# Rotated stores on another queue, and the output's first operand in two transfers with its low parts last

## The chip, the cores and the metric

The kernel runs on one core of a Trainium2 chip. The metric is the device time of one execution in microseconds (us), lower is better. The kernel before was timed in three runs; the profile comes from a separate execution, taken with the hardware profiler.

## The reference, cut to what matters

One decoder block on a sequence of 2048 positions and 1024 channels, in float32:

```python
proj = h @ w_in[l]                      # eight parts of 1024 columns
x_rnn, z_rnn, q, k, v, z_attn, g_r, g_a = jnp.split(proj, IN_SPLITS, axis=-1)
hr = rg_lru(causal_depthwise_conv(x_rnn, ...), ...)
y_rnn = (hr * silu(z_rnn)) @ w_out_rnn[l]
qh = apply_partial_rope(q.reshape(B, S, N_HEADS, HEAD_DIM), cos, sin)   # 32 of a head's 128 columns turn
kh = apply_partial_rope(k.reshape(B, S, N_HEADS, HEAD_DIM), cos, sin)
o = dilated_attention_mixture(qh, kh, vh).reshape(B, S, D_ATTN)
y_attn = (o * silu(z_attn)) @ w_out_attn[l]
merged = sigmoid(g_r + bg_r) * y_rnn + sigmoid(g_a + bg_a) * y_attn
x = x + gate[:, None, :] * (merged @ w_o[l])
return rms_norm(x, g_final)
```

What matters here is the turn from `proj` to the attention and to the product with `w_out_rnn`, whose input, hr times silu(z_rnn), is the tensor `yaT`.

## The kernel before

**Numbers.** Every float32 operand is split into a high part (rounded, by ScalarE, `hi_act`, line 162) and a low part (the rest, by GpSimd, `lo_pool`, line 168, or VectorE, `lo_dve`, line 171). A product of two operands is three matmuls on TensorE (`mm3`): high by high, high by low, low by high. All matmuls have line 154. On TensorE's part of the profile, "LDWEIGHTS" (PEld) loads a 128 by 128 block and "MATMUL" (PE) streams 512 columns past it.

**Projections.** They run in two passes over halves of the sequence (`f` = 0, then 1). In a pass there are 28 pairs of column blocks, in the order of `pair_order`; each pair is one Strassen step of seven products (`strassen`), and a product is twelve matmuls (four blocks of the contraction, three matmuls each). The seven products of a pair read the operands B11, T2, T3, T1, B21, T4 and B22 of the normalised input, each as a high and a low tile `T`. Those tiles lie in a pool of 14 slots; a slot is free for another tile when the last pair's product has read it, B11's two slots first. The last product of a pair (B22) is issued behind the first of the next pair. The counter `n_prod` counts issued products over both passes, 196 in each. Work that goes with the products is put into lists by that count: `steps_after` and `late` for steps of evictions, `after_prod` for others; `run_late` runs what is due after each product, first `late`, then `after_prod`, then the operands of coming pairs (`pump`).

The weights are tiles `S` in a ring of seven slots. In the second pass most come back ready split from the scratch `sD`, by SyncE's queue (SP, line 334), and some raw, split four products ahead of their use; those of the pairs 22 and 27 (the last one) are built anew: raw loads `R` (line 257), sums on VectorE (lines 298 to 312), high parts on ScalarE and low parts on GpSimd.

**Evictions.** A pair gives four tiles of 128 by 512. The last six pairs of a pass are plain q, rotated q, plain, rotated k, plain, plain (`TAIL_ROTATED`). A rotated tile goes through a shuffle (VectorE, line 1157), two products (GpSimd, line 1158, and VectorE, line 1161), a sum (VectorE, line 1165) and a store of four transfers, one for each head's 32 rows (line 1170), the sum and the store being one product apart. A plain tile is stored in two or so transfers (line 1200). An eviction that needs no sum is made by ScalarE (line 1134), the others by VectorE (line 482). All these stores are issued by SP. ScalarE's queue issues the stores of `oD` in the second pass (lines 1353 and 1354), the scaled `w_o`, which is loaded as `wo` by SP (line 1335).

**Queues.** SP and ScalarE issue their transfers in the order of the program and wait, at each, for what it needs. ScalarE's transfers stand in line with its arithmetic. The compiled program gives each transfer one of eight completion semaphores in turn, in program order over both queues, so a transfer also waits until the eighth before it has landed.

**The turn.** After the product that frees the slot of a weight tile, `load_free` calls `load_next`. When the 196 weights of the pass are through, it goes on with what the output needs: the first weights of `w_out_rnn` from the scratch `wD` into the first slots of the ring (`load_wd`, line 367), four 128 by 512 tiles of `yaT` into the slots `R` (`load_yd`, line 373), and, at the second call, the other four blocks of `yaT` in one transfer into a slot `T` (line 345). It begins behind the last pair's second product (T2), when the last of that pair's weights is made.

**The output.** `steps` is a generator of output tiles: for each tile, eight blocks of the contraction, three matmuls each, into a PSUM tile `pj`. It is spent in pieces between the parts of the attention: the first 18 blocks, two tiles and a quarter, come before the attention's first scores. Ahead of the first tile, `split_y(0, k)` splits the eight blocks of the first operand, high part `yh` on ScalarE, low part `yl` on VectorE. Each tile takes two weight tiles of the ring's four slots, one for each half of the contraction; the load into a slot (`load_w`, again line 367) waits until TensorE has read the tile that was there. In the first tile the three matmuls of a block stand together: high, high by low, low by high.

**The attention** loads k and q of a head (`kraw`, lines 1522 and 1523), splits them into `kq`, and its first scores need the first of four such parts, its second group of scores all four. Its tiles are laid over the slots that the projections used: k's and q's second and third loads lie over the slot `T` that held the four blocks of `yaT`, and the buffers of `yh` lie in part over those of `wo`.

Of the kernel before, what the change touches and what calls it, by code (L numbers as in the profile page):

```python
# [10 lines left out]
F32 = mybir.dt.float32  # L11
# [9 lines left out]
P = 128  # L21
# [68 lines left out]
def decoder_block(ctx, tc, x, c, positions, g_norm, w_mod, b_mod, w_in, b_gate, conv_w, conv_b,  # L90
# [4 lines left out]
    def T(pool, shape, dt, tag, **kw):  # L95
        cnt[0] += 1
        return pool.tile(shape, dt, tag=tag, name=f"{tag}_{cnt[0]}", **kw)
# [228 lines left out]
    def load_next():  # L326
        n = n_loaded[0]
        n_loaded[0] += 1
        if n < 28 * 7:
            t = s_tile([P, 2, KH, P])  # L330
            if is_raw(n // 7, n % 7):
                unsplit.append((n, t, loaders[n // 7](*PLAIN[n % 7])))
            else:
                nc.sync.dma_start(t[:].bitcast(F32), sD[n])
            loaded.append((n, t))
        else:
            k = n - 28 * 7
            if k < 3:
                load_wd(0, 0, k) if k < 2 else load_wd(0, 1, 0)
            if k < 4:  # L340
                load_yd(yaT, 0, k)
            if k == 1:

                t = T(hp, [P, KH, CH], F32, "T", bufs=14)
                nc.sync.dma_start(t[:], yaT[KH * P :, :CH].rearrange("(k p) j -> p k j", p=P))
                for i in range(KH):
                    Y0[True, 0, KH + i] = t[:, i, :]


    def load_free():  # L350
        n = n_loaded
# [17 lines left out]
    def load_yd(ys, n, k):  # L369
        x = n_y[0]  # L370
        n_y[0] += 1
        t = T(pR, [P, CH], F32, f"R{x % 4}")
        nc.sync.dma_start(t[:], ys[k * P : (k + 1) * P, n * CH : (n + 1) * CH])
        Y0[ys is yaT, n, k] = t
# [767 lines left out]
    def rotated_pairs(qp, f, Ct, St):  # L1142

        for base, dstT, qs in QK:
            made = [0]

            def rotated(i, j, ps, u, dstT=dstT, qs=qs, made=made):
                n = 2 * f + j
                cq = slice(j * CH, (j + 1) * CH)
                t0 = T(qp, [P, CH], F32, "t0", bufs=NT0)  # L1150
                wait, v = scaled(t0, ps, u, qs), []
                wait += (0, 1, 2, 2)[made[0]]
                made[0] += 1

                def shuffle():
                    v.append(T(qp, [P, CH], F32, "t1", bufs=NT1))
                    nc.vector.stream_shuffle(v[0][:], t0[:], swap)
                    nc.gpsimd.tensor_tensor(t0[:], t0[:], Ct[:, cq], ALU.mult)

                def turn():  # L1160
                    nc.vector.tensor_tensor(v[0][:], v[0][:], St[:, cq], ALU.mult)

                def add():
                    t1 = v[0]
                    nc.vector.tensor_tensor(t1[:], t1[:], t0[:], ALU.add)

                def store():
                    for hh in range(4):
                        r0 = (4 * i + hh) * P
                        nc.sync.dma_start(dstT[r0 : r0 + 32, :, n * P : (n + 1) * P],  # L1170
                                          v[0][hh * 32 : (hh + 1) * 32, :].rearrange("p (r j) -> p r j", r=4))

                steps_after(n_prod[0], ((wait, shuffle), (wait + 1, turn), (wait + 2, add), (wait + 3, store)))

            strassen(qp, f, (base, "rotated"), rotated)
            yield
# [145 lines left out]
    def gated_weight(ep):  # L1322

        gate_b = T(ep, [P, D], F32, "gb")
        nc.sync.dma_start(gate_b[:], gateD[0:1, :].broadcast_to([P, D]))
        tt = nc.vector.tensor_tensor

        def group(k):
            v = {}

            def load():
                for i in range(2):
                    v[i] = T(ep, [P, 2, CH], F32, "wo", bufs=2)
                    rows = slice((i * KH + k) * P, (i * KH + k + 1) * P)
                    nc.sync.dma_start(v[i][:], w_o[0, rows, :].rearrange("p (j c) -> p j c", j=2))

            def gate(i):
                tt(v[i][:].rearrange("p j c -> p (j c)"), v[i][:].rearrange("p j c -> p (j c)"), gate_b[:], ALU.mult)

            def sums(i):  # L1340
                if not i:
                    v["t"] = T(ep, [P, 2, CH], F32, "ws")
                t = v["t"]
                (b11, b12), (b21, b22) = ((v[i][:, 0, :], v[i][:, 1, :]) for i in range(2))
                if not i:
                    tt(t[:, 0, :], b12, b11, ALU.subtract)
                    tt(t[:, 1, :], b22, t[:, 0, :], ALU.subtract)
                else:
                    tt(b22, b22, b12, ALU.subtract)
                    tt(b21, b21, t[:, 1, :], ALU.subtract)  # L1350

            def store_sums():
                nc.scalar.dma_start(oD[k, :, :2, :], v["t"][:])
                nc.scalar.dma_start(oD[k, :, 2:, :], v[1][:])

            return ((0, load), (4, lambda: gate(0)), (5, lambda: gate(1)), (6, lambda: sums(0)),
                    (7, lambda: sums(1)), (8, store_sums))

        for k, i in enumerate((1, 11, 21, 31)):
            for d, fn in group(k):  # L1360
                later(i + d, fn)
# [53 lines left out]
    for f in range(2):  # L1415
        if f:
            pools.close("xp")
            vx = pools.open("vx", bufs=1)
            second_values()
        else:  # L1420
            first_values()
        pools.close("vx")
        plain = plain_pairs(f)
        rp = pools.open("rp", bufs=1)
        touch(rp, (("u1", 1), ("u2", 2), ("u3", 1), ("xc", 2), ("y", 2), ("gi", 1), ("a", 1), ("t", 1),
                   ("gh", 1, 2, P), ("gl", 1, 2, P), ("xh", 1), ("xl", 1)))
        plain_pool[0] = rp
        plain_at[0] = lambda: T(rp, [P, CH], F32, "ev", bufs=3)
        bigr = reset_rows(rp, f)
        gates = gate_pairs(rp, f)  # L1430
        rotary_tables(rp, f)
        if f:
            output_weights()
            for x, (_, pieces) in enumerate(pair_order()):
                if x in ANEW:
                    events.extend((28 * 7 + 7 * x + d - LEAD, 15 * x + i, fn)
                                  for i, (d, fn) in enumerate(operand_events(x, pieces, f)))
            events.sort(key=lambda e: e[:2])

        pump()  # L1440
        n = 0
        for m in range(KT):
            recurrent(rp, bigr, f, m)
            for _ in range(others[m]):
                next(plain if is_plain(n) else gates)
                n += 1
        last_product()
        finish_late()
        pools.close("rp")
        qp = pools.open("qp", bufs=1)  # L1450
        plain_pool[0] = qp
        plain_at[0] = lambda: T(qp, [P, CH], F32, "t0", bufs=NT0)

        touch(qp, (("u1", 1), ("u2", 2), ("u3", 1), ("t0", NT0), ("t1", NT1)))
        tabs = load_tables(qp, f)
        if f:
            gated_weight(qp)
        else:
            xp = pools.open("xp", side="right", bufs=1)
            x0 = next_norm()  # L1460
        rotated = rotated_pairs(qp, f, *tabs)
        for n, r in enumerate(TAIL_ROTATED):
            if n == len(TAIL_ROTATED) - 1 and f == 0:
                next_even()
            next(rotated if r else plain)
        last_product()
        finish_late()
        for n in sorted(after_prod):
            run_late(n)
        pools.close("qp")  # L1470
# [341 lines left out]
    def steps(jobs):  # L1812
# [55 lines left out]
        def split_y(j, k):  # L1868
            if j < len(jobs):
                w, ys, n = jobs[j]  # L1870
                t = Y0.pop((ys is yaT, n, k), None)
                yh, yl = Y.get((j, k)) or new_y(j, k)
                t = yl[:].bitcast(F32) if t is None else t[:]
                hi_act(yh[:], t)
                on_dve = k not in (3, 4) if j == LAST_HEAD else k % 2 or not j
                (lo_dve if on_dve else lo_pool)(yl[:], t, yh[:])

        def load_g(t):
# [22 lines left out]
        for k in range(KT):  # L1901
            split_y(0, k)
        yield
        last = None
        for t, (j, m) in enumerate(tiles):
            ps = T(pj, [P, CH], F32, "pj") if j < LAST_HEAD or t % 4 < 2 else FP["bank"](t % 4 - 2)
            for k in range(KT):
# [18 lines left out]
                wt = W[x]  # L1926
                row = {5: 7, 6: 5, 7: 6}.get(k, k) if t == TURN + 1 else k
                yh, yl = Y[j, row]
                mm3(ps[:], wt[:, 0, row % KH, :], wt[:, 1, row % KH, :], yh[:], yl[:], first=k == 0, last=k == KT - 1)
                if k % KH == KH - 1 and (j != LAST_HEAD if m < KT - 1 else j <= LAST_HEAD):  # L1930
                    W.pop(x)

# [390 lines left out]
```

## Time and profile before

| | |
|---|---|
| median of three runs | 2206.31 us (2204.77 to 2211.26) |
| the profiled execution's own time | 2207.36 us |
| its span, first to last instruction | 2205.6 us |
| mean granted clock of TensorE | 0.993 |
| transfers | 513.90 MB, mean 233 GB/s |

Times in a profile are us from the start of the span. Rows of a timeline hold start, duration, engine, line, operation, output<-input, shapes, the number of merged instructions, and in brackets the idle time before and what ended it. "SPq" and "ACTq" rows are transfers being issued; the duration is that of the issue, not of the transfer. "DMA to landing" gives the time from issue until the last byte's semaphore (least, median, most). Rows of a waits view hold who waited for whom, us in total, times, the longest. Rows of the windows view hold the stretch, its length, the busy time and number of instructions of PE, PEld, VectorE (DVE), ScalarE (ACT) and GpSimd (POOL), the granted clock of TensorE, the mean busy share of the 16 DMA engines, and GB/s.

### The profile page before, as it was taken

To read this page: it belongs to the slowest core of one execution; us is meant where nothing else is said; L and a number is where in the kernel's file an instruction comes from. 1 tells how busy PE (TensorE), PEld (TensorE's weight loads), DVE (VectorE), ACT (ScalarE), POOL (GpSimd) and SP (SyncE) were. 2 spreads that over 40 slices of the span, in tenths; PEclk is the share of its full clock that TensorE was granted. 3 is DMA by queue.
4 is the path that set the end of the run, shared out by engine and by line. 5 is a ranking of instruction groups with operands and counts; after the bars stand their busy time and mean duration, and the time that the engine had idled before them with its cause. 6 is when DMAs were issued, how large, how long until landed. Compare 5 with 4: busy or idle time off the path is not lost. (4 is left out here: it accounts for less than half of the span.)

```text
span 2205.6 us, 34316 instructions
## 1 busy us (share of the span) xinstructions
PE 2167.7 (98%) x11358; PEld 1842.8 (84%) x11359; DVE 1490.4 (68%) x2455; ACT 1262.0 (57%) x2538; POOL 1238.5 (56%) x910
## 2 busy tenths in 40 slices
PE   8999999999999999999999999999999999999998
PEld 5898888888888998888888887888889898978786
DVE  5578888978667665455545456466677878755876
ACT  3546667677543437666567412567677887633433
POOL 2368767777667346445544323456565656433986
PEclk9999999999999999999999999999999999999999
DMA  8355665665897657787887899989988888799553
GB/s 279 97 158 182 217 211 173 207 223 191 238 284 207 203 174 246 256 247 245 256 255 247 254 296 273 295 266 287 277 275 266 241 261 254 223 293 297 171 164 134
DMA packets 454233, 513.90 MB, mean 233 GB/s; under 512 B 91208, under 2 KB 333604, under 8 KB 453032
## 3 DMA queue, kind: packets, MB, share of 16 engines
q1 hardware_dynamic: 427156, 431.81, 65.6%
q10 hardware_dynamic: 26708, 79.86, 9.4%
q8 instruction: 90, 1.47, 0.3%
q14 instruction: 87, 0.71, 0.1%
q0 software_dynamic: 192, 0.05, 0.0%
HBM read 337.52 MB, written 174.07 MB: 232 GB/s over the span
## 5 line engine op out<-in xcount | busy, mean ns | idle before, releaser
L168 POOL TENSOR_TENSOR S<-R,S 128x512 fp32r<-128x512 f32 x278 | 412.7, 1490 | 390.1 <-ACT S L162 340.5
L154 PE MATMUL V<-T,S 128*128 128x512 f32 x1344 | 324.4, 390 | 0.7 <-DVE xr L482 0.7
L154 PE MATMUL X<-T,S 128*128 128x512 f32 x1344 | 323.3, 389 | 0.2 <-POOL S L168 0.2
L154 PEld LDWEIGHTS X<-T,S 128*128 128x128 f32 x1344 | 252.0, 188 | 52.8 <-POOL S L168 0.7
L154 PEld LDWEIGHTS V<-T,S 128*128 128x128 f32 x1344 | 251.4, 188 | 53.0 <-DVE xr L482 1.1
L154 PE MATMUL pj<-yh,S 128*128 128x512 f32 x848 | 288.6, 398 | 5.0 <-ACT yh L162 3.4
L162 ACT ACTIVATE S<-R 128x512 fp32r<-128x512 f32 x278 | 171.3, 622 | 120.5 <-DMA R<-in_w_in_dram 98.8
L168 POOL TENSOR_TENSOR S<-s,S 128x512 fp32r<-128x512 f32 x114 | 181.6, 1593 | 98.1 <-ACT S L162 76.8
L154 PEld LDWEIGHTS pj<-yh,S 128*128 128x128 f32 x848 | 161.5, 191 | 38.4 <-ACT yh L162 4.3
L1575 ACT ACTIVATE pp<-pp,st 128x256 f32<-128x256 f32 (+3 forms) x256 | 133.4, 523 | 75.3 <-DVE st L1574 74.9
L154 PE MATMUL pj<-yl,S 128*128 128x512 f32 x424 | 168.1, 397 | 2.5 <-DVE yl L171 1.6
L154 PE MATMUL Y<-T,S 128*128 128x512 f32 x672 | 161.6, 389 | 0.0
L154 PE MATMUL W<-T,S 128*128 128x512 f32 x672 | 161.5, 389 | 0.0
L154 PE MATMUL Z<-T,S 128*128 128x512 f32 x672 | 161.4, 389 | 0.0
L154 PEld LDWEIGHTS Z<-T,S 128*128 128x128 f32 x672 | 126.1, 188 | 26.2
L154 PEld LDWEIGHTS Y<-T,S 128*128 128x128 f32 x672 | 126.1, 188 | 26.2
L154 PEld LDWEIGHTS W<-T,S 128*128 128x128 f32 x672 | 126.1, 188 | 26.1
L162 ACT ACTIVATE S<-s 128x512 fp32r<-128x512 f32 x114 | 71.1, 624 | 112.1 <-DVE s L299 57.6
L977 DVE SCALAR_TENSOR_TENSOR xc<-xr,par,xc 128x512 f32<-128x512 f32 x96 | 99.9, 1040 | 51.3 <-ACT xc L971 49.1
L171 DVE TENSOR_TENSOR ptl<-pT,pth 128x384 fp32r<-128x384 f32 (+1 forms) x160 | 97.8, 628 | 49.4 <-ACT pth L162 47.2
L1574 DVE CUSTOM_DVE_ANT_0 pp<-sc,msk 128x256 f32<-128x256 f32 (+3 forms) x256 | 104.2, 449 | 36.3 <-PE sc L154 34.1
L168 POOL TENSOR_TENSOR kq<-kraw,kq 128x512 fp32r<-128x512 f32 (+1 forms) x64 | 101.2, 1591 | 40.3 <-ACT kq L162 40.3
(391 smaller groups left out, 4838.6 us busy)
## 6 DMA issues: line engine op xcount, KB each, us to landing
sD<-S ACTq DMA_DIRECT2D x112, 512.0 KB, 3.8
S<-sD SPq DMA_DIRECT2D x112, 512.0 KB, 5.2
S<-wD SPq DMA_DIRECT2D x100, 512.0 KB, 5.8
R<-in_w_in_dram SPq DMA_DIRECT2D x195, 256.0 KB, 4.2
wD<-s ACTq DMA_DIRECT2D x64, 256.0 KB, 4.2
T<-in_w_mod_dram SPq DMA_DIRECT2D x8, 1024.0 KB, 12.2
vN<-ev SPq DMA_DIRECT2D x64, 128.0 KB, 2.8
zaT<-ev SPq DMA_DIRECT2D x32, 256.0 KB, 3.3
```

Source lines behind the costliest of these rows:

```text
L154: nc.tensor.matmul(o, lhsT=l, rhs=r, start=st, stop=sp, **kw)
L162: nc.scalar.activation(o, i, AF.Copy)
L168: nc.gpsimd.tensor_tensor(o, i, h.bitcast(F32), ALU.subtract)
L171: nc.vector.tensor_tensor(o, i, h.bitcast(F32), ALU.subtract)
L977: nc.vector.scalar_tensor_tensor(xc, xr[:, i : i + CH], cw(i), xc, ALU.mult, ALU.add)
L1574: nc.vector.tensor_tensor_reduce(pdst, s_ps, mask, 1.0, 3e38, ALU.add, ALU.min, m_)
L1575: nc.scalar.activation(pdst, pdst, AF.Exp, bias=m_, scale=-1.0, accum_out=l_)
```

## The change

Three things change, all at the turn.

In the second pass the rotated tiles' stores, four transfers for each of eight tiles, are issued by ScalarE instead of SP, at the same place in the program.

The first operand of the output, `yaT`'s first 512 columns, is no longer loaded by `load_next` in four small transfers and a large one, but by a function `load_first_y` of its own in two transfers of four blocks each, both into slots `T`. It is put into `after_prod` at the count 385, behind the last pair's first product, the last that reads B11.

In the first tile of the output, only two matmuls of each block are made in turn, those that read `yh`; the eight that read `yl` are kept in a list and come behind the last block. The low parts of the blocks 0 and 2 of this operand go to GpSimd, those of the six others stay on VectorE.

```diff
@@ load_next
             if k < 3:
                 load_wd(0, 0, k) if k < 2 else load_wd(0, 1, 0)
-            if k < 4:
-                load_yd(yaT, 0, k)
-            if k == 1:
-
-                t = T(hp, [P, KH, CH], F32, "T", bufs=14)
-                nc.sync.dma_start(t[:], yaT[KH * P :, :CH].rearrange("(k p) j -> p k j", p=P))
-                for i in range(KH):
-                    Y0[True, 0, KH + i] = t[:, i, :]
-
+
+    def load_first_y():
+
+        for half in range(2):
+            t = T(hp, [P, KH, CH], F32, "T", bufs=14)
+            nc.sync.dma_start(t[:], yaT[half * KH * P : (half + 1) * KH * P, :CH].rearrange("(k p) j -> p k j", p=P))
+            for i in range(KH):
+                Y0[True, 0, half * KH + i] = t[:, i, :]
@@ rotated_pairs, store
-                        nc.sync.dma_start(dstT[r0 : r0 + 32, :, n * P : (n + 1) * P],
+                        (nc.scalar if f else nc.sync).dma_start(dstT[r0 : r0 + 32, :, n * P : (n + 1) * P],
                                           v[0][hh * 32 : (hh + 1) * 32, :].rearrange("p (r j) -> p r j", r=4))
@@ the second pass
         if f:
             gated_weight(qp)
+            after_prod.setdefault(2 * 28 * 7 - 7, []).append(load_first_y)
@@ steps, split_y
-                on_dve = k not in (3, 4) if j == LAST_HEAD else k % 2 or not j
+                on_dve = k not in (3, 4) if j == LAST_HEAD else k % 2 or not j and k > 2
@@ steps
-        last = None
+        last, low = None, []
...
-                mm3(ps[:], wt[:, 0, row % KH, :], wt[:, 1, row % KH, :], yh[:], yl[:], first=k == 0, last=k == KT - 1)
+                ws = [wt[:, i, row % KH, :] for i in range(2)]
+                if t:
+                    mm3(ps[:], *ws, yh[:], yl[:], first=k == 0, last=k == KT - 1)
+                else:
+                    for i in range(2):
+                        mm(ps[:], ws[i], yh[:], k == i == 0, False)
+                    low.append((ws[0], yl))
+                while low and k == KT - 1:
+                    wh, yl = low.pop(0)
+                    mm(ps[:], wh, yl[:], False, not low)
```

## The prediction

> **What bounds the kernel now.** I read the page's head and its first part first, then the idle time of PE around the place that the diff touches, then the two queues that feed it. The profiled execution took 2207.36 us, 1.8 us more than its span; the median of the three runs shown, 2206.31 us, is 1.05 us below it.
>
> ```profile
> span 2205.6 us, 34316 instructions
> PE 2167.7 (98%) x11358; PEld 1842.8 (84%) x11359; DVE 1490.4 (68%) x2455; ACT 1262.0 (57%) x2538; POOL 1238.5 (56%) x910
> ```
>
> TensorE is busy for 98% of the span, so a change can only win what PE idles, or runs slowly, at the place it touches. The edits meet at the turn, 1341 to 1392 us: the last pair of the projections, then the output's first tile (24 matmuls into `pj`). The windows view has PE, its granted clock and the DMA engines there (PE, PEld, DVE, ACT, POOL busy; clock; DMA share; GB/s):
>
> ```profile
> 1347.00:1351.00 4.00, 4.00 (x20) 3.30 (x19) 4.00 (x3) 0.60 (x1) 4.00 (x3) 1.00 0.70 163
> 1351.00:1356.00 5.00, 5.00 (x24) 4.14 (x23) 4.97 (x5) 0.63 (x1) 4.23 (x3) 1.00 0.52 112
> 1361.00:1366.00 5.00, 5.00 (x24) 4.14 (x23) 0.69 (x1) 1.17 (x2) 0.00 (x0) 1.00 0.98 356
> 1366.00:1372.00 6.00, 2.12 (x9) 1.12 (x7) 2.03 (x4) 1.39 (x3) 0.00 (x0) 1.00 1.04 398
> 1374.00:1376.00 2.00, 2.00 (x6) 1.61 (x5) 1.69 (x3) 0.58 (x2) 0.00 (x0) 0.50 1.05 228
> ```
>
> Until 1366 PE does not idle, while the DMA engines are half empty (112 GB/s); then PE works 2.12 of 6 us with the DMA engines full, and by 1374 its clock is halved. The chain of waits shows what twelve matmuls take, the timeline of PE gives the price, and the waits view names who ended it:
>
> ```profile
> 2069.52 2.72 PE W L154 x12
> ```
>
> ```profile
> 1366.18 0.39 PE L154 MATMUL pj<-yh,S 128*128 128x512 f32 x1
> 1367.72 0.50 PE L154 MATMUL pj<-yl,S 128*128 128x512 f32 x1 [1.16 <-DVE yl L171]
> 1371.88 0.50 PE L154 MATMUL pj<-yh,S 128*128 128x512 f32 x1 [2.72 <-ACT yh L162]
> 1372.61 0.71 PE L154 MATMUL pj<-yl,S 128*128 128x512 f32 x1 [0.22 <-DVE yl L171]
> ...
> 1376.36 0.40 PE L154 MATMUL pj<-yl,S 128*128 128x512 f32 x1
> ```
>
> ```profile
> ACT yh L162 <- DMA R<-yaT: 8.4, 3, 4.2
> ```
>
> Sixteen matmuls start from 1366.18 until the one at 1376.36. At 0.227 each (2.72 / 12) that one was due at 1366.18 + 16 × 0.227 = 1369.81: **6.55 us lost**, 4.10 in the three gaps and 2.45 in slow matmuls. Behind it stand ACT's high parts, and behind these the loads of `yaT`. That is all there is to win: 0.30%.
>
> In the windows above the clock fell to 0.50 after gaps of 1.16 and 2.72 us. The Trainium skill, "TensorE: Matmul & The Clock Gate" (What's actually happening), has the clock drop to half only after about 3.4 us of idling. By that rule of the Trainium skill no gap here costs clock, and 4.10 us could go instead of 6.55; the measurement differs and decides.
>
> **The change part by part.** Both queues first, SP's timeline and ACT's (start, duration, line, transfer or instruction).
>
> ```profile
> 1340.77 0.43 SPq L1335 DMA_DIRECT2D wo<-in_w_o_dram  x1
> 1341.60 5.09 SPq L1170 DMA_DIRECT2D kT<-t  x8
> 1349.41 3.42 SPq L1170 DMA_DIRECT2D kT<-t  x4
> 1355.56 0.55 SPq L367 DMA_DIRECT2D S<-wD  x1
> 1358.69 0.51 SPq L345 DMA_DIRECT2D T<-yaT  x1
> 1365.27 8.39 SPq L1200 DMA_DIRECT2D kT<-t  x8
> 1377.09 0.38 SPq L367 DMA_DIRECT2D S<-wD  x1
> ```
>
> ```profile
> 1342.88 0.63 ACT L162 ACTIVATE S<-R 128x512 fp32r<-128x512 f32 x1 [1.78 <-DVE R L307]
> 1343.42 0.58 ACT L1134 ACTIVATE t<-X 128x512 f32<-128x512 f32 x1
> 1344.42 1.14 ACT L162 ACTIVATE S<-R 128x512 fp32r<-128x512 f32 x2
> 1357.61 0.33 ACTq L1354 DMA_DIRECT2D oD<-wo  x1
> 1360.93 0.60 ACT L1134 ACTIVATE t<-X 128x512 f32<-128x512 f32 x1 [7.84 <-PE X L154]
> 1372.41 2.17 ACT L162 ACTIVATE yh<-T 128x512 fp32r<-128x512 f32 x4
> ```
>
> *Stores to ACT.* 32 transfers of the second pass leave SP. Twenty of them lie ahead of 1341, under a busy PE: 0. Twelve are the x8 and the x4 above, 8.51 us of SP. Of these twelve the profile says:
>
> ```profile
> L1170 SPq DMA_DIRECT2D kT<-t x12: 549/598/1527, 1341.6 to 1352.2; - x12
> DMA to landing us min/median/max: 2.1/3.3/4.3
> ```
>
> On ACT I price each at 0.60 us, their median (ACT's own issues show 0.33): 12 × 0.60 = 7.2 us, between 4.0 and 8.5. Queued behind them on ACT are the last pair's high parts (1342.88 to 1345.56) and the eviction L1134 at 1343.42. A transfer also waits until the eighth before it has landed (section on the kernel); the third tile's last two so wait for the `wo` loads, issued until 1340.77. Their landing, the last pair's last product and POOL's last low part:
>
> ```profile
> DMA to landing us min/median/max: 4.8/4.8/4.8
> 1363.46 2.88 PE L154 MATMUL V<-T,S 128*128 128x512 f32 x12
> 1353.49 1.74 POOL L168 TENSOR_TENSOR S<-s,S 128x512 fp32r<-128x512 f32 x1
> ```
>
> 1340.77 + 4.8 = 1345.6, so ACT's high part of 1342.88 goes to about 1346.2, L1134 ends at 1347.4 and, behind the fourth tile's store, the last high part of 1344.42 ends near 1351.4. POOL's low parts at 1.74 each then end near 1356, against 1355.2. The last pair's seventh product starts at 1363.46, the third (4 × 2.72 ahead) at 1352.58: each keeps 4 us or more. Cost 0; cover gone, it is the slower rival.
>
> *The first operand in two transfers.* The four R loads and the one T load of 1356 to 1362 become two of 1 MB behind the last pair's first product, which reads B11. It starts seven products ahead of the one at 1363.46 (the last of the pair before lies between), at 1344.42, and ends near 1347.3. SP now waits there for the store that reads L1134's tile (1347.4) and for landings: I place the first at 1349.8, between 1347.3 and 1355.6 (SP no earlier than now). The operand is 1024 × 512 × 4 bytes, 2.1 MB; at 300 GB/s, between the 163 of the emptier windows and the 398 of the full one, that is 7 us: in by 1357; by the time that the T load of 1358.69 took, 10.3 us, by 1360.1. Both lie ahead of ACT, free at 1361.5 after L1134. The bytes are the same; half empty engines carry them.
>
> *High parts.* Eight at 0.54 (2.17 / 4). The second one's buffer lies where `wo` lay until its store (issued 1357.61) has landed:
>
> ```profile
> DMA to landing us min/median/max: 8.3/8.3/8.3
> ```
>
> 1357.61 + 8.3 = 1365.9, and earlier if the engines are emptier, so the last high part ends between 1365.9 and 1369.8, and PE wants it at 1366.18 + 14 × 0.227 = 1369.36: 0 to 0.45 us, I take 0.3.
>
> *Low parts last, two of them on POOL.* No matmul is added. Sixteen with yh cover 3.63 us. DVE's last eviction and its low parts, in the timeline of DVE:
>
> ```profile
> 1366.38 0.69 DVE L482 TENSOR_TENSOR t<-V,u 128x512 f32<-128x512 f32 x1 [2.03 <-PE V L154]
> 1373.20 2.49 DVE L171 TENSOR_TENSOR yl<-T,yh 128x512 fp32r<-128x512 f32 x4
> ```
>
> Six at 0.62 from 1367.07 end at 1370.8; the last is due at 1371.4 or later. POOL idles since 1355.2. Cost 0; on DVE alone the eight would end at 1372.0, 0.6 late. The first tile thus wins 6.55 − 0.3 = 6.25.
>
> *What is late next.* Tile 2 starts 48 matmuls after the first tile, in this profile near 1376.36 + 32 × 0.227 = 1383.6, with weights issued at 1377.09. The next such load took:
>
> ```profile
> L367 SPq DMA_DIRECT2D S<-wD x1: 376/376/376, 1378.7 to 1378.7; - x1
> DMA to landing us min/median/max: 6.6/6.6/6.6
> ```
>
> PE did not wait for the one of 1377.09, so that one took less than 1383.6 − 1377.1 = 6.5 us; I say 6.2 to 6.6. Now tile 2 is due at 1366.18 + 0.3 + 4 × 2.72 = 1377.4. Its slot is free after the 20th matmul instead of the 12th (1370.9 against 1369.1), and SP gets there 3.4 us after its last kT store (1365.27 + 8.39 to 1377.09). That store needs DVE's eviction (1367.07) and a landing, so I end it at 1368.3: issue 1371.7, landing 1377.9 to 1378.3. PE waits 0.5 to 0.9 us; I take 0.75. The K and Q loads stand in the same queue and come forward by the same 5.4 us, so the attention's first waits stay as they are. **Sum: 6.55 − 0.3 − 0.75 = 5.5 us**; own range 4.5 to 6.2. Span 2205.6 − 5.5 = 2200.1; the median becomes 2206.31 − 5.5 = 2200.8.
>
> **The rivals.** *All of it:* weights of tile 2 land in 5.5 us because the engines are emptier; then only the 0.3 stays, 6.25 to 6.55 us: 2199.8 to 2200.1. For it: most of `yaT` leaves the full stretch. Against: its queue still follows the kT stores.
>
> *The DMA engines bind:* weights, stores and `yaT` share the same engines, and every transfer moves forward only as far as the first big one does. If SP issues it at 1353 instead of 1349.8, all comes 2.5 us earlier (1355.56 − 1353) and the gain is about that: 2203.8. For it: a share of 1.04 and landings of 8 to 10 us. Against: 112 GB/s right before. The Trainium skill, "DMA: Bandwidth & Descriptors" (Issuing engines are not separate DMA queues), says that another issuing engine saves only issue time; the trace agrees in that the L1170 stores cost SP 8.51 us. By that rule the stores' move gives nothing once the engines are full.
>
> *It does not do what it says:* the first transfer goes out where L367 stood, since its eighth predecessor is late; same time, 2206.3.
>
> *Slower:* ACT is held by the landings of its own stores. An earlier group of the same stores shows how long:
>
> ```profile
> L1170 SPq DMA_DIRECT2D kT<-t x4: 549/556/1077, 1331.8 to 1335.1; - x4
> DMA to landing us min/median/max: 5.9/7.0/8.3
> ```
>
> With 8.3 instead of some 3 us twice over, the fourth store ends near 1360, the fifth and sixth products of the last pair (1358.02, 1360.74) wait for high and low parts until about 1362.7: 4.7 us of gap and, as above, about 2.4 of half clock, 7.1 against 5.5 won: 2207.9. It decides once ACT is held beyond about 1354. Against it: the twelve after 1341 landed in 2.1 to 4.3 us.
>
> **How the numbers follow.** Forecast 0.52, all of it 0.20, the engines bind 0.17, no effect 0.05, slower 0.06. The range goes to 2205.0 above, which leaves out the last two cases, and to 2198.9 below, the largest gain and 0.9 us of scatter (the runs shown spread from 2204.77 to 2211.26). 0.3%, 6.6 us, is about what a measurement of this kernel can tell from no change; that edge is 2199.7, just beyond all that PE loses here. Faster by more takes the best case and scatter: 0.22; slower by more than 0.3% 0.05; within it 0.73.
>
> **What would show it.** Right: PE's gap before the sixth or seventh matmul of `pj` gone and the clock at 1.00 around 1372; two T loads on SP near 1350; the windows around 1351 fuller; PE's one new wait, below 1.2 us, at tile 2 on a DMA of S. Wrong: a gap in the products ahead of 1366 ended by ACT or POOL S (ACT held); T loads after 1353; `yh` high parts after 1370; PE waiting on `yl`, or on kq for the first scores longer than now.

## The result, and the profile after

The changed kernel takes 2200.96 us in the median of 15 runs (2199.66 to 2206.5), the kernel before, beside it on the same chips, 2205.88 us (2203.86 to 2211.95). The ratio is 0.9979 with a 95% interval of [0.9972, 0.9986]: 4.6 us (3.1 to 6.2) by the ratio, 4.9 by the medians. The forecast was 5.5 us, to 2200.8. The profiled execution took 2200.95 us. First the head of its page:

```profile
span 2198.8 us, 34316 instructions
PE 2164.6 (98%) x11359; PEld 1840.8 (84%) x11359; DVE 1484.9 (68%) x2453; ACT 1261.1 (57%) x2538; POOL 1241.4 (56%) x912
```

The spans of the two profiled executions differ by 6.8 us, more than the medians; that of before lay 1.5 us above its own median (2207.36 against 2205.88). So the turn is read by itself. The windows, in the places of those shown of before (PE, PEld, DVE, ACT, POOL busy; clock; DMA share; GB/s):

```profile
1347.00:1351.00 4.00, 4.00 (x19) 3.34 (x18) 4.00 (x3) 1.64 (x3) 3.65 (x3) 1.00 0.92 235
1351.00:1356.00 5.00, 5.00 (x23) 4.14 (x23) 4.96 (x7) 0.63 (x1) 3.07 (x2) 1.00 1.06 369
1361.00:1366.00 5.00, 5.00 (x23) 4.13 (x22) 0.69 (x1) 3.43 (x7) 2.18 (x2) 1.00 1.02 379
1366.00:1372.00 6.00, 6.00 (x28) 4.98 (x27) 4.30 (x7) 1.44 (x3) 0.37 (x1) 1.00 0.77 191
1374.00:1376.00 2.00, 2.00 (x11) 1.65 (x10) 0.00 (x0) 0.40 (x2) 1.28 (x1) 1.00 0.75 218
```

The work of the DMA engines has moved from behind 1366 to ahead of 1356 (369 GB/s where there were 112), TensorE works 6.00 of 6 us instead of 2.12, and the clock stays at 1.00. TensorE's timeline and its waits:

```profile
1363.74 2.88 PE L154 MATMUL V<-T,S 128*128 128x512 f32 x12
1366.46 3.79 PE L154 MATMUL pj<-yh,S 128*128 128x512 f32 x16
1370.09 1.98 PE L154 MATMUL pj<-yl,S 128*128 128x512 f32 x8
...
1377.96 0.47 PE L154 MATMUL pj<-yh,S 128*128 128x512 f32 x1 [0.46 <-DMA S<-wD]
...
1415.34 0.93 PE L1672 MATMUL pT<-cs,pp 128*128 128x128 f32 x7
```

```profile
PE pj L154 <- DMA S<-wD: 0.5, 1, 0.5
PE sc L154 <- POOL q L1536: 0.3, 1, 0.3
```

The first tile has no gap: 24 matmuls in 5.44 us (1366.46 to 1371.90). Tile 2 waits for its weights, once. To measure the turn I take the start of the last product (V) and that of a fixed later group, the first transposes `pT` of this kind, 245 matmuls behind the output's first. In the kernel before, the latter is

```profile
1420.70 0.93 PE L1672 MATMUL pT<-cs,pp 128*128 128x128 f32 x7
```

so the stretch took 1420.70 − 1363.46 = 57.24 us, and takes 1415.34 − 1363.74 = 51.60: **5.64 us won at the turn**. The table below gives the same for every run; each such value comes from a single execution. What feeds TensorE, on the timelines of SP, ScalarE, GpSimd and VectorE (from 346 to some 1450 the changed kernel's line numbers are one less than before's: L366, L1169 and L1199 are the loads of `wD` and the rotated and plain stores):

```profile
1342.40 4.89 SPq L1199 DMA_DIRECT2D kT<-t  x6
1347.39 1.54 SPq L345 DMA_DIRECT2D T<-yaT  x2
...
1353.20 5.96 SPq L366 DMA_DIRECT2D S<-wD  x4
1359.27 9.30 SPq L1199 DMA_DIRECT2D kT<-t  x8
...
1371.69 0.38 SPq L366 DMA_DIRECT2D S<-wD  x1
```

```profile
1345.09 2.95 ACTq L1169 DMA_DIRECT2D kT<-t  x4
1348.09 1.15 ACT L162 ACTIVATE S<-R 128x512 fp32r<-128x512 f32 x2 [4.09 <-DMA kT<-t]
...
1361.71 0.62 ACT L162 ACTIVATE yh<-T 128x512 fp32r<-128x512 f32 x1
1363.68 3.76 ACT L162 ACTIVATE yh<-T 128x512 fp32r<-128x512 f32 x7 [1.35 <-DMA oD<-wo]
```

```profile
1352.34 1.73 POOL L168 TENSOR_TENSOR S<-s,S 128x512 fp32r<-128x512 f32 x1
```

```profile
1367.27 3.69 DVE L171 TENSOR_TENSOR yl<-T,yh 128x512 fp32r<-128x512 f32 x6
```

### The profile page after: what moved, and what is told of

Read it like the earlier page. It is cut to its first block, busy times and chain, and to the rows that moved or that the text cites. A ratio compares the mean times of both kernels' runs of the same rounds, so it can differ in the third digit from the quotient of the medians.

```text
span 2198.8 us, 34316 instructions
## 1 busy us (share of the span) xinstructions
PE 2164.6 (98%) x11359; PEld 1840.8 (84%) x11359; DVE 1484.9 (68%) x2453; ACT 1261.1 (57%) x2538; POOL 1241.4 (56%) x912
## 4 chain that ended last, share of the span: by engine, by line
PE 60%; DMA 7%; DVE 4%; issue 3%; POOL 2%; ACT 2%; SPq 1%; ACTq 0%; POOLq 0%; DVEq 0%
PE X L154 12%; PE V L154 11%; PE pj L154 9%; PE Z L154 6%; PE W L154 6%; PE Y L154 6%; PE o L154 3%; PE sc L154 3%; PE pg L154 1%; DMA or<-oD 1%; PE pT L1659 1%; DMA meT<-fg 1%; DMA fg<-mrT 1%; PE pT L1672 1%; DMA or<-in_w_o_dram 1%
## 5 line engine op out<-in xcount | busy, mean ns | idle before, releaser
L1639 ACT ACTIVATE pp<-pp,M 128x256 f32<-128x256 f32 (+3 forms) x256 | 118.0, 524 | 9.3 <-DVE M L1763 9.3
```

What stands on the lines that cost most here:

```text
L1639: nc.scalar.activation(pp, pp, AF.Copy, scale=w)
```

## The experiments

Theory: the first operand's two loads decide, by how far ahead of the last product they go out; the freed slots let them go at 1347.3, and only if SP's queue is not still issuing stores then. Rivals: one part alone carries the gain (the slots, the stores, or the order of the low parts); or the stores' move gives nothing, as it saves only issue time.

All runs in one table: the ratio to the kernel before with its interval, the gain that it means ((1 − ratio) × 2207 us), the gain at the turn in the profiled execution (57.24 minus its stretch), and the lead, from the issue of the first T load to the start of the last product.

| parts | ratio | gain, us | at the turn | lead |
|---|---|---|---|---|
| none (before) | 1 | 0 | 0 | 4.8 (R from 7.3) |
| all three (the change) | 0.9979 [0.9972, 0.9986] | 4.6 | 5.6 | 16.4 |
| stores | 0.9992 [0.9983, 1.0001] | 1.8 | 1.9 | 8.5 (four R loads 9.9 to 0.9) |
| loads | 1.0000 [0.9991, 1.0009] | 0.0 | −0.6 | 8.1 |
| low parts | 1.0004 [0.9996, 1.0013] | −0.9 | −3.3 | 1.5 (R from 5.2) |
| loads, low parts | 0.9991 [0.9982, 1.0000] | 2.0 | 1.3 | 10.5 |
| stores, loads | 0.9975 [0.9965, 0.9986] | 5.5 | 5.8 | 16.4 |
| stores, low parts | 0.9993 [0.9984, 1.0002] | 1.5 | 1.9 | 8.6 (R from 10.0) |
| all, stores of k only | 0.9980 [0.9972, 0.9988] | 4.4 | 5.0 | 13.7 |
| all, eight idle issues | 0.9992 [0.9983, 1.0000] | 1.8 | 1.5 | 10.5 |
| all, mask on ScalarE | 0.9978 [0.9968, 0.9988] | 4.9 | 5.9 | 15.8 |
| all, every store on ScalarE | 1.0003 [0.9994, 1.0013] | −0.7 | 0.5 | 15.9 |
| loads, low parts, stores merged | 1.0024 [1.0014, 1.0034] | −5.3 | 1.1 | 8.9 |

**Loads and low parts, the stores back on SP.**

```diff
-                        (nc.scalar if f else nc.sync).dma_start(dstT[...]
+                        nc.sync.dma_start(dstT[...]
```

> The changed kernel with the rotated stores put back on SyncE; the two loads and the low parts' order stay as changed. Theory (the stores decide when SyncE's queue is free): the loads go out near 1354 instead of 1347.4, the first tile loses about 0.3 us, and tile 2's weights go out so late that TensorE waits some 4 us for them: 1.6 us faster than the kernel before (1 to 3), 3 us slower than the changed one. Rival (stores on another engine save only issuing time, which nothing waits for): the same as the changed kernel, 4.9 us faster.

SP's timeline of this run, what SP waited for from 1338 to 1351, and TensorE's two gaps:

```profile
1338.49 5.18 SPq L1169 DMA_DIRECT2D kT<-t  x8
1343.77 2.52 SPq L1199 DMA_DIRECT2D kT<-t  x4
1346.39 3.21 SPq L1169 DMA_DIRECT2D kT<-t  x4
1349.69 1.23 SPq L1199 DMA_DIRECT2D kT<-t  x2
1351.02 1.13 SPq L345 DMA_DIRECT2D T<-yaT  x2
```

```profile
SPq L1169 <- DVE u L420: 0.4, 1, 0.4
SPq L1199 <- DVE s L312: 0.3, 1, 0.3
```

```profile
1365.42 3.91 PE L154 MATMUL pj<-yh,S 128*128 128x512 f32 x16 [1.03 <-ACT yh L162]
...
1379.34 0.50 PE L154 MATMUL pj<-yh,S 128*128 128x512 f32 x1 [2.76 <-DMA S<-wD]
```

2.0 us instead of 4.6: without the stores' move more than half of the gain is gone. SP issues 18 transfers in 12.5 us with only 0.7 us of waiting; it is simply busy issuing, and the loads come out behind. The two gaps stand where they were expected, the first larger (1.03 for 0.3), the second smaller (2.76 for 4).

Two waits behind 1351, one of SP and one of ScalarE, carry the delay to TensorE:

```profile
SPq L366 <- DMA T<-yaT: 7.6, 2, 5.0
```

```profile
1364.22 3.76 ACT L162 ACTIVATE yh<-T 128x512 fp32r<-128x512 f32 x7 [4.12 <-DMA oD<-wo]
```

SP's third and fourth load of output weights stand eight transfers behind the two T loads and waited until these had landed, the slower one after 11.8 us; what follows on SP, tile 2's weights among it, is late by that. In the changed kernel both had landed by 1357.6, and its trace has no such wait. The first gap is not a wait for the T loads: the second high part stood until 1364.22 behind the landing of the store to `oD`, which took 9.0 us here and 7.2 in the changed kernel.

**Eight idle issues.** To see whether it was the issuing or what was issued, eight transfers of next to no bytes stand ahead of the loads in the changed kernel.

```diff
     def load_first_y():
 
+        dm = T(hp, [P, 8, 4], F32, "dm", bufs=1)
+        for i in range(8):
+            nc.sync.dma_start(dm[:16, i, :], yaT[P * i : P * i + 16, :4])
```

> The changed kernel with eight more transfers on SyncE right ahead of the first operand's two loads: 16 rows of 16 bytes each, into a tile that nobody reads, so nearly no bytes and nothing to wait for. Eight is the number of completion semaphores, so every later transfer keeps its own. Theory (issue time on SyncE's queue is what the stores cost there): at 0.4 to 0.6 us each the two loads go out 3 to 5 us later (1351 to 1352 instead of 1347.4), tile 2's wait grows from 0.6 to 2 us or more, and the gain falls from 4.9 to between 2 and 3.5 us. Rival (what the stores cost there is their bytes, or the data they wait for): the loads go out 1 us later at most in effect, and the gain stays at 4.5 to 5.

SP and TensorE of this run:

```profile
1347.51 4.68 SPq L345 DMA_DIRECT2D dm<-yaT  x8
1352.29 0.94 SPq L348 DMA_DIRECT2D T<-yaT  x2
```

```profile
1366.84 3.91 PE L154 MATMUL pj<-yh,S 128*128 128x512 f32 x16 [1.22 <-ACT yh L162]
...
1380.50 0.76 PE L154 MATMUL pj<-yh,S 128*128 128x512 f32 x1 [2.49 <-DMA S<-wD]
```

The same two gaps as with the stores on SP, behind the same two waits (SP 7.9 us for the T loads, the second high part until 1365.56), and the same gain, 1.8 us for 2.0, at the same lead. Of the 4.68 us some 1.3 were waits for completions of ScalarE's stores, by the waits view, the rest issuing at 0.42 in the median. So a delay of the loads in SP's queue is enough to cost the time. The rival, that the stores' bytes or data cost it, fails: the same stores move in this run and in the change, on ScalarE.

**Stores and loads, the low parts as before.** The third part of the diff is undone.

> The changed kernel with the low parts in their old place and on their old engines. Theory (the load's time is what counted, the low parts' order hardly): the gap of about 1.2 us at the first tile, where TensorE waits for a low part behind VectorE's last eviction, comes back in whole or in part, but tile 2's wait of 0.6 us for its weights takes that much less: 4 to 4.9 us faster than the kernel before, within 0.9 us of the changed kernel. Rival (the order of the low parts carries the gain): 1 to 3 us faster than before.

```profile
1366.85 0.50 PE L154 MATMUL pj<-yl,S 128*128 128x512 f32 x1 [1.16 <-DVE yl L171]
```

5.5 us, by the intervals not to be told from the whole change. The gap of 1.16 us is back in full, and it is the only one: tile 2 no longer waits, since it comes that much later while its weights do not. The order of the low parts moved a wait and won nothing that these times show.

**Each part alone.** The same diffs, two parts undone at a time.

> The kernel before with only the twelve rotated stores of the second pass that stand ahead of the turn issued by ScalarE; the output's first operand is still one transfer into its old slot, and the low parts keep their old order. Theory (the order of SyncE's queue sets when the first operand goes out): with the stores gone from SyncE's queue the load goes out about 2.5 us earlier (near 1353 instead of 1355.6), behind VectorE's last eviction, so the time falls by about 2 us. Rival A (moving stores saves only the issuing time of a queue that has time): 0, within 0.3 us. Rival B (the stores are the whole change): 5 us faster.

> The kernel before with only the first operand's load in two transfers into the freed slots; stores stay on SyncE, low parts keep their old order. Theory: the two loads go out near 1354, since stores still stand ahead of them; the gap of 1.2 us at the first tile (TensorE waiting for a low part) stays, the gap of 2.7 us goes or shrinks below 1, and tile 2 waits some 4 us for its weights, because everything of SyncE's queue behind the loads is as late as before; 1.6 us faster (0.5 to 3). Rival (the slots are the whole change): 4.5 to 5.5 us faster.

> The kernel before with only the first tile's low parts last, and those of the blocks 0 and 2 on GpSimd. Theory: the gap of 1.16 us, TensorE waiting for a low part, goes; the gap of 2.7 us, where it waits for the high part of a late block, grows by what TensorE is earlier there; nothing is won, 0 (-1 to 1). Rival (the order of the low parts is worth its 1.2 us by itself): 1.2 to 2 us faster.

Loads alone, TensorE and SP's waits from 1320 to 1368:

```profile
1368.49 0.77 PE L154 MATMUL pj<-yh,S 128*128 128x512 f32 x1 [3.31 <-DMA S<-wD]
```

```profile
SPq L366 <- DMA T<-yaT: 7.9, 2, 4.7
```

(The run of the stores moves all 32 of the second pass, not only the twelve that its expectation names, and the operand's load that it leaves alone is five transfers.) The stores gave 1.8 us as expected, though the interval just includes a ratio of 1. The gaps were 1.16, 1.02 and 0.22 us at the first tile and 0.75 at tile 2. The loads gave nothing, and not by way of tile 2, as expected, but at the first weights: a load that goes out only 8 us ahead puts 2.1 MB in front of the output's weights (TensorE waited 3.31 us for the first), and the third and fourth weight load, eight transfers behind the two T loads, waited for their landing (7.9 us). The low parts alone gave nothing, as expected; in the profiled execution, which at 2211.45 us lay 2.6 us above the run's median, the gaps became larger:

```profile
1368.57 1.07 PE L154 MATMUL pj<-yh,S 128*128 128x512 f32 x2 [1.84 <-ACT yh L162]
1373.31 5.67 PE L154 MATMUL pj<-yh,S 128*128 128x512 f32 x12 [3.67 <-ACT yh L162]
```

**Stores and low parts, without the loads.**

> The changed kernel without the two transfers: stores on ScalarE and low parts last, but the first operand again in four small loads and one large one into their old slots, behind the weights' loads in SyncE's queue. Theory (the freed slots let the load stand ahead of the last stores and of the weights): the last operand blocks land near 1369 as with the stores alone; since the low parts no longer stand in the way, the first tile loses 1.0 to 2.5 us instead of 2.9, tile 2's wait of 0.7 stays: 2 to 3.5 us faster than before. Rival (the stores' move frees the queue, and the slots hardly matter): 4.5 to 5 us.

ScalarE's timeline of this run:

```profile
1367.57 1.30 ACT L162 ACTIVATE yh<-R 128x512 fp32r<-128x512 f32 x2 [4.21 <-DMA R<-yaT]
```

1.5 us, below the 2 to 3.5 that were expected: the third high part waits for the last small loads, which landed at 1367.5 and 1368.2. So neither stores nor loads do it alone: 0 to 2.0 us against 4.6 and 5.5. Whether they need one another beyond that is open. With the low parts in their old order, stores give 1.8, loads 0 and both 5.5, 3.7 more than the sum; with the low parts moved, counted from their −0.9, stores add 2.4, loads 2.9 and both 5.5, hardly more than the sum. Each of these gains has some 2 us to either side.

**The stores of k only.** In the changed kernel, q's stores, some 40 us ahead, go back to SP.

```diff
-                        (nc.scalar if f else nc.sync).dma_start(dstT[...]
+                        (nc.scalar if f and qs == 1.0 else nc.sync).dma_start(dstT[...]
```

> The changed kernel with ScalarE issuing only the rotated stores of k (16 transfers, twelve of them in the stretch that the prediction counted); those of q, some 40 us ahead of the turn, stay on SyncE. The prediction gave the stores far ahead of the turn a value of 0. If so, the time is that of the changed kernel, 4.9 us faster than before (within 0.9); if moving them off SyncE also pulled the queue forward at the turn, the loads go out later than 1347.4 and 1 us or more is lost.

4.4 us, within the interval of the change. In this execution the loads went out 2.6 us less ahead (one had waited 1.0 us for a store to land), and 0.7 us was missing at the turn, 0.42 of it a wait for the second high part, which stood until 1365.48 behind the store to `oD`. Stores far ahead are worth little or nothing; more can't be told apart here.

**The mask on ScalarE.** One more transfer leaves the stretch of SP's queue ahead of tile 2's weights.

```diff
-    nc.sync.dma_start(msk[:], cst[:, K_M23:])
+    nc.scalar.dma_start(msk[:], cst[:, K_M23:])
```

> The changed kernel with one more transfer moved from SyncE to ScalarE: the mask's load, which stands between the last stores and the loads of k, q and tile 2's weights. If tile 2's wait of 0.6 us comes from the place of its weights in SyncE's queue, its issue comes about 0.6 us earlier and the wait goes to 0 to 0.1: 0.5 us faster than the changed kernel. If the wait is set by the DMA engines' load, the weights land no earlier and nothing changes.

```profile
1376.07 0.47 PE L154 MATMUL pj<-yh,S 128*128 128x512 f32 x1 [0.16 <-DMA S<-wD]
```

The wait went from 0.46 to 0.16 us and the turn wins 5.9 instead of 5.6: place in the queue, again. The time, 0.9978, is not to be told from the change's 0.9979.

**Every store on ScalarE.** The plain tiles' stores of the second pass too.

```diff
-                            nc.sync.dma_start(dstT[r0 : r0 + m, :, n * P : (n + 1) * P],
+                            (nc.scalar if f else nc.sync).dma_start(dstT[r0 : r0 + m, :, n * P : (n + 1) * P],
```

> The changed kernel with the plain tiles' stores of the second pass issued by ScalarE too. This is the slower rival made real: ScalarE's high parts of the first operand then stand behind a store that needs VectorE's last eviction (1367.35). Theory: the high parts start near 1368.6, TensorE waits about 2 us at the output's first tile, and the gain falls from 4.9 to 2 to 3 us. If another queue for the stores is always a gain: as the changed kernel, or 0.5 faster.

ScalarE and TensorE:

```profile
1364.73 4.46 ACTq L1199 DMA_DIRECT2D kT<-t  x6
1369.23 4.28 ACT L162 ACTIVATE yh<-T 128x512 fp32r<-128x512 f32 x8 [4.92 <-DMA kT<-t]
```

```profile
1369.92 5.52 PE L154 MATMUL pj<-yh,S 128*128 128x512 f32 x16 [4.61 <-ACT yh L162]
```

The whole gain is gone, not the half of it that was expected: behind six stores the high parts start at 1369.2 instead of 1361.7, though the loads had gone out as early as in the change. ScalarE's queue then is what SP's was.

**Merged stores.** Stores on SP, but each tile in one transfer for four heads.

```diff
-                    for hh in range(4):
-                        r0 = (4 * i + hh) * P
-                        nc.sync.dma_start(dstT[r0 : r0 + 32, :, n * P : (n + 1) * P],
-                                          v[0][hh * 32 : (hh + 1) * 32, :].rearrange("p (r j) -> p r j", r=4))
+                    heads = dstT[4 * i * P : 4 * (i + 1) * P, :, n * P : (n + 1) * P].rearrange("(h p) r j -> h p r j", h=4)
+                    nc.sync.dma_start(heads[:, :32], v[0][:].rearrange("p (r j) -> p r j", r=4))
```

> The changed kernel with the rotated stores of the second pass back on SyncE, but each tile's four transfers merged into one of four heads: the same bytes, on the same queue, in a quarter of the transfers. Theory (SyncE's queue is full of issuing ahead of the first operand's load: in the run with the stores back on SyncE it issued 26 transfers back to back from 1338.5 to 1353.4, 0.57 us each): nine issues fewer, 5.1 us, if a merged one costs no more than a single one, so the loads go out near 1346 to 1347 and the gain is that of the changed kernel, 4.9 us; if a merged one's issue costs in proportion to its rows, nothing is saved and it stays at 2. Rival (what counts is that another queue takes the stores, or what the stores wait for): as with the stores on SyncE, 2 us faster than before, 3 slower than the changed kernel.

The merged stores' issues near the turn (ns, least, median, most), and the DMA engines' mean busy share, in tenths, in 40 slices from 1350 to 1354:

```profile
L1169 SPq DMA_DIRECT2D kT<-t x3: 570/571/4159, 1345.6 to 1355.4; - x3
```

```profile
DMA  2223222322232223222322232222322232223222
```

Slower by 5.3 us; both theories missed. The issue is as cheap as hoped, 0.57 us for a whole tile, but while it runs the 16 engines are busy at a mean of 0.2 to 0.3 (some 87 GB/s): by the trace's semaphore events the merged ones landed after 7 to 10 us. Ahead of the turn TensorE waited 3.1 us for parts of weights, and at the turn the loads were late all the same. The expectation also miscounts SP's issues; there were 22 to 1353.4. On the question at hand this run is inconclusive: it saved issues and paid for them with landings. The idle issues answer it.

## Why the prediction was right, point by point

- **What bounds: right.** The 6.55 us lost at the first tile are gone: it takes 5.44 us, 24 at 0.227. No run won more than 5.9 at the turn, under that cap.
- **Stores at no cost: right, but their time was taken too low.** The last four took 2.95 us on ScalarE, 0.74 each against the 0.60 taken, and the twelve 10.05 us with their waits, more than the 8.5 of the upper bound. They began early enough for it: the last high part of that group ended at 1349.2 (forecast 1351.4), GpSimd's low part at 1354.1 (1356). The cover was real, but not unlimited: with the plain stores too it was gone. The stores far ahead at 0: supported, for the sixteen of q.
- **First load at 1349.8: too late by 2.4 us.** It went out at 1347.39, at the lower bound: I let SP wait for a store and for landings there, and it waited only 0.2 us for the slot. Both had landed by 1357.6 (by the trace's events; forecast 1357 to 1360.1).
- **High parts: the wait was there, the loss was not.** The second waited for the store to `oD` until 1363.68 and not 1365.9: it was issued 1.15 us earlier and landed in 7.2 us instead of 8.3. 0 lost instead of 0.3. That the loads ahead shortened its landing is not shown: with loads as far ahead it took 8.4 us (mask) and 8.6 (stores, loads).
- **Low parts at 0: right as far as it went.** They ended at 1370.96 (forecast 1370.8), no gap. That this part won nothing was not forecast: undoing it costs a gap of 1.16 us and saves the wait at tile 2.
- **Tile 2 late by 0.75: right.** Issue 1371.69 (forecast 1371.7), landing after 6.1 us by the trace's events, start 1377.96 instead of 1377.34: 0.62.
- **The sum.** 6.55 − 0 − 0.62 = 5.93 against 5.5; 0.25 of it was lost again at the second scores, which waited for GpSimd's `q` (not foreseen), which leaves 5.68; 5.64 was measured. The comparisons give 4.6, with 3.1 to 6.2. That 5.5 lies so near is in part luck: 0.3 (high parts) and 0.13 (tile 2) more than forecast stand against 0.25 of a wait that the forecast did not have. The first load's 2.4 us did not count, since the second high part waited longer, for the store to `oD`. In the profiled execution 0.7 more was given back near 1441, by the clock (last section).
- **"The DMA engines bind": its condition did not come.** Where it came, its price was near: with the stores on SP and with the idle issues the lead was 10.5 us, which is 1353.0 on the clock of the kernel before, and the gains were 2.0 and 1.8 us against the 2.5 that it gives for 1353. The T loads then took up to 11.8 us to land, and SP's and ScalarE's waits, shown above, passed that on. That full engines alone set these landings was not tested. Its conclusion that the stores' move gives nothing was wrong: without the move 2.0 of 4.6 us are left, and nothing of 5.5 with the low parts in their old order. The rule quoted there from the Trainium skill, "DMA: Bandwidth & Descriptors" (Issuing engines are not separate DMA queues), agrees with the idle issues, where a delay by issuing cost as much as the stores on SP did. Its consequence here was not nothing, since issue time was what was short: 18 transfers held SP for 12.5 us.
- **"Slower": the place was right.** ScalarE held by its own stores took the whole gain once the plain ones joined. With the change's stores alone it waited too, 4.45 and 4.09 us ahead of high parts, but only until 1348.1, short of the 1354 from which that rival counts.

## What to carry to other kernels

Where a large load misses its moment although the DMA engines ahead of it are half empty, count the issues that stand in front of it in its queue: at some 0.6 us each, a dozen small stores hide 7 us. Free the slot and the queue in one edit; either alone gave 0 to 2.0 us, both together 4.6 and 5.5. Look also at what waits for the load's completion semaphore: in this program a load that lands late holds the eighth transfer behind it. The engine that takes the stores pays the same price, so stop before its own next due work.

## What the hardware showed that was not expected

**Short gaps that halve the clock, and longer ones that do not.** The changed kernel's windows near 1441, behind a gap of 1.41 us (1438.70 to 1440.11), and TensorE in the run with the stores of k only:

```profile
1440.00:1441.00 1.00, 0.89 (x6) 0.92 (x7) 0.71 (x4) 0.18 (x2) 0.00 (x0) 0.76 0.98 324
1441.00:1443.00 2.00, 2.00 (x7) 1.61 (x7) 1.82 (x11) 1.35 (x5) 0.00 (x0) 0.50 0.90 321
1443.00:1444.00 1.00, 1.00 (x4) 0.81 (x3) 0.75 (x7) 1.00 (x6) 0.74 (x2) 0.54 0.35 133
```

```profile
1437.09 0.49 PE L154 MATMUL sc<-sm,msk 128*128 128x128 f32 x2 [2.59 <-DVE sm L1727]
1437.33 0.48 PE L154 MATMUL pj<-yh,S 128*128 128x512 f32 x1
```

After 1.41 us the clock stood at 0.50 for about 3.4 us (0.48 + 2 + 0.92, if it is either 0.50 or 1.00), which costs an estimated 1.7 us, half of that; after 2.59 us it stayed at 1.00. The kernel before has the same gap of 1.41 at its place, without the halving. So the length of a gap does not decide alone. The Trainium skill, "TensorE: Matmul & The Clock Gate" (What's actually happening), describes a free-running window of about 3.4 us whose activity sets the clock. The length of the slow stretch agrees with it; the halving after 1.41 us does not agree with the idle window that its table names for the drop. A gap that falls half into each of two windows would explain why a longer one was harmless, but that was not tested. In the two executions, of before and after, the same gap cost 0 and about 1.7 us.

**A store whose outer dimension is 4 used a quarter of the engines** (mean share 0.2 to 0.3, above). By the trace's semaphore events, the data of each merged store came in with four completions, those of a weight load of 128 rows with sixteen. The Trainium skill, "DMA: Bandwidth & Descriptors" (Why a DMA increments its semaphore by 16 and not by 1), has the number of engines follow from the slowest dimension of both sides; the run agrees, with four completions for the outer dimension of 4.
